# First feed-forward of a two-layer hybrid trunk: the fifth quad's weight forms made first, the norm taken later, and the rows of 1/rms made by two float32r products

## The chip, the cores and the metric

The kernel runs on one core of one Trainium2 chip. The metric is the device time of one execution in microseconds (us); three runs of the kernel before are given, and one execution was profiled.

## What is computed

Two layers, each a half-step SwiGLU feed-forward, a mixer of three head groups, and a second half-step feed-forward, all behind an RMS norm; a last RMS norm ends it. Here 512 positions of width 1024, feed-forward width 2816, all float32. The change is in the first feed-forward and in the norm that its six stages share.

```python
def _rmsnorm(x, g):
    y = xf * lax.rsqrt(jnp.mean(xf * xf, axis=-1, keepdims=True) + EPS)
    return (y * g.astype(jnp.float32)).astype(x.dtype)

def _swiglu(x, w_gate, w_up, w_down):
    return (jax.nn.silu(x @ w_gate) * (x @ w_up)) @ w_down

# in each layer
x = x + MACARON * _swiglu(_rmsnorm(x, ffn1_norm), ffn1_w_gate, ffn1_w_up, ffn1_w_down)
```

## The kernel before

**Tiling.** x stands transposed: 8 tiles of 128 features by 512 positions, held as four pairs `xp[m]`. A float32 product is made of three float32r products: each operand is split into a high part (a cast on ScalarE, L89) and a low part (a subtraction on VectorE, L90); `parts` is this pair. Every weight that reaches TensorE costs these two instructions.

**Quads.** The 22 column tiles of the gate and of the up matrix are taken in 22 *quads*: quad q covers two column tiles, of the gate for even q and of the up matrix for odd q. A quad is computed by a fast 2 by 2 block scheme: seven products n = 1 to 7 of half size (12 matmuls of 128x256 each, `product`, L281 to L283) in place of eight. Its weights come as raw blocks (`fetch`; for quad 4 of the very first feed-forward `fetch_apart`) and are made into forms in three steps (`forms_steps`): `direct` (tile `wd`, for n = 1, 2, 3), `first` (a sum, L148, and tile `wa`, for n = 7 and 6), `second` (a sum, L154, and tile `wb`, for n = 5 and 4). The tiles `wa` and `wb` share three buffers (tag `w2`), `wd` has two.

**Leaving PSUM.** After each product `after` copies or adds PSUM into the quad's tile `c`: n = 1 copies on ScalarE (L353), n = 2 adds on VectorE (L355), n = 6 and 5 copy on ScalarE (L357, L359), n = 7 and 3 subtract on VectorE (L361, L363), n = 4 copies on ScalarE (L365). n = 1, 6, 7 and 4 use one bank (`pa`), so n = 6 must wait for the copy after n = 1, and n = 7 for the copy after n = 6. Tiles `c` of even quads have the tag `g`, of odd quads `u`, two buffers each.

**The norm.** The features are not normalised before the product; the gate and up columns are multiplied by 1/rms afterwards. `squares(m)` squares a pair on ScalarE (L237, into a tile with the tag `u`) and adds it to `acc` on VectorE (two adds for each pair, the first pair one: seven adds, L240 and L243). `norm_columns` sums over partitions with four products with a column of ones (`pss`, L250) and takes the power on GpSimd (`rc`); `norm_rows` turns that into a tile of rows: four diagonals on VectorE (L264), four float32 products of 128x128 with a tile of ones (`psr`, L265), a copy (`rr`, L267). It is called six times in the program. `done(q)` then multiplies a gate by `rr` (L374), applies Silu, multiplies again (L376); for an odd quad it multiplies by the gate (L379) and splits the result into `h`.

**The first feed-forward.** In `start`, quads 0 and 1 are computed plainly (the `pg` products, while x and weights still arrive), with ScalarE's and VectorE's order written by hand up to the forms of quads 2 and 3. From there the order of the rest is set by the list `steps` in `gate_up` (times 7 q + `WHEN[n]`, some moved), by the list `norms` (one entry is called between the matmuls and the `after` of each product) and by a scheduler that puts each engine's instructions in a fixed order. The squares follow the copies of quads 0 and 1; `norm_columns` comes with the tenth product, `norm_rows` and `done(0)`, `done(1)` with the twelfth.

Of the kernel before, what the change touches and what calls it, by code (L numbers as in the profile page):

```python
# [9 lines left out]
F32 = mybir.dt.float32  # L10
F32R = mybir.dt.float32r
AF = mybir.ActivationFunctionType
ALU = mybir.AluOpType
AX = mybir.AxisListType

P = 128
D = 1024
T = 512
# [9 lines left out]
KP = KT // 2  # L28
# [20 lines left out]
def trunk(ctx, tc, xt, w_first, w_gu1, w_dn1, w_in, w_out, w_gu2, w_dn2, w_last, par, con, wst, bst, gvr, gain, out):  # L49
    nc = tc.nc  # L50
    cpool = ctx.enter_context(tc.tile_pool(name="cpool", bufs=1))
# [1 line left out]
    wpool = ctx.enter_context(tc.tile_pool(name="wpool", bufs=1))  # L53
    spool = ctx.enter_context(tc.tile_pool(name="spool", bufs=2))
    pp = ctx.enter_context(tc.tile_pool(name="pp", bufs=8, space=bass.MemoryType.PSUM))
    stage = {}

    def bank(name):
        return pp.tile([P, T], F32, tag="ps", name=name)
# [1 line left out]
    def big(name, dt=F32):  # L61
        return stage["pool"].tile([P, 2 * T], dt, tag="h", name=name, bufs=11)
# [3 lines left out]
    def uniq(s):  # L66
        uid[0] += 1
        return f"{s}{uid[0]}"
# [8 lines left out]
    ones = cpool.tile([P, P], F32, name="ones")  # L77
# [2 lines left out]
    nc.vector.memset(mhalf, -0.5)  # L80
    table = cpool.tile([P, 1], F32, name="table")
    nc.scalar.copy(table, mhalf[:, 0:1])
    ident = cpool.tile([P, P], F32, name="ident")
    make_identity(nc, ident)


    def parts(hi, lo, src):

        nc.scalar.copy(hi, src)  # L89
        nc.vector.tensor_tensor(lo, src, hi.bitcast(F32), ALU.subtract)  # L90

    def load(src):
        n = src.shape[-1] * (src.shape[1] if len(src.shape) == 3 else 1)
# [79 lines left out]
    split = parts  # L173


    state = {}
    warm_ps = bank("warm")
    xf = [None] * KP

# [6 lines left out]
    def xl(k):  # L186
        return xf[k // 2][:, 2 * T + (k % 2) * T : 2 * T + (k % 2 + 1) * T]

    def scratch(i, name):

        if stage["tags"] is None:
            return big(uniq(name))
        if i == 2:
            return stage["pool"].tile([P, 4 * T], F32, tag="hp", name=uniq(name), bufs=4)
        return stage["pool"].tile([P, 2 * T], F32, tag=stage["tags"][i], name=uniq(name), bufs=2)

    def gained(m, k, gcol, hi, lo, c):
# [59 lines left out]
    def norm_rows():  # L257

        rc = state["rc"]
        pr = bank(uniq("psr"))  # L260
        dg = scratch(2, "dg")
        for n in range(NCH):
            d = dg[:, n * P : (n + 1) * P]
            nc.vector.tensor_scalar(d, ident, rc[:, n : n + 1], None, ALU.mult)  # L264
            nc.tensor.matmul(pr[:, n * P : (n + 1) * P], lhsT=ones, rhs=d, start=True, stop=True)  # L265
        rr = spool.tile([P, T], F32, tag="rr", name=uniq("rr"), bufs=1)
        nc.scalar.copy(rr, pr)  # L267
        state["rr"] = rr
# [39 lines left out]
    def gate_up(w_gu, first, others, tail, from_start=False):  # L308
# [7 lines left out]
        quads = [(p, j) for p in range(FP) for j in range(2)]  # L316
        steps = [(7 * q + t, 0, q, n) for q in range(len(quads)) for n, t in WHEN.items()]
        if from_start:
            moved = {(3, 1): 15.3, (3, 2): 15.6, (2, 4): 27.5}
            steps = [(moved.get((q, n), t), k, q, n) for t, k, q, n in steps]  # L320
        steps += [(t, 1, None, work) for t, work in others]
        steps.sort(key=lambda e: e[:2])
        live, gates, raws = {}, {}, {}
# [25 lines left out]
        def after(q, n):  # L349
            c11, c21, c12, c22 = [quarter(q, i) for i in range(4)]  # L350
            b = live[q]
            if n == 1:
                state["copied"] = nc.scalar.copy(c11, b["pa"])  # L353
            elif n == 2:
                nc.vector.tensor_tensor(c11, b["pb"], c11, ALU.add)  # L355
            elif n == 6:
                state["copied"] = nc.scalar.copy(c12, b["pa"])  # L357
            elif n == 5:
                state["copied"] = nc.scalar.copy(c22, b["pc"])  # L359
            elif n == 7:  # L360
                nc.vector.tensor_tensor(c22, c22, b["pa"], ALU.subtract)  # L361
            elif n == 3:
                nc.vector.tensor_tensor(c12, b["pc"], c12, ALU.subtract)  # L363
            else:
                nc.scalar.copy(c21, b["pa"])  # L365
                done(q)

        def done(q):
            p, j = quads[q]
# [18 lines left out]
        else:  # L388
            begin(0)
            begin(1)  # L390
            for m in range(KP):
                for q in (0, 1):
                    for n in (1, 2):
                        ps = psum(q, ("pa", "pb")[n - 1])
                        hi, lo = live[q]["w"][n]
# [23 lines left out]
    def start(live, done, ahead, raws_of):  # L419

        for k in range(12):
            warm = warm_ps[:, (k % 4) * P : (k % 4 + 1) * P]
            nc.tensor.matmul(warm, lhsT=ones, rhs=ones, start=True, stop=True)
        pool = stage["pool"]
        extra = pool.tile([P, 4 * T], F32R, tag="hp", name="a21", bufs=4)
        a21 = [(extra[:, m * H : (m + 1) * H], extra[:, (4 + m) * H : (5 + m) * H]) for m in range(KP)]
        raws = [wpool.tile([P, 1024], F32, tag="pt", name=uniq("rawp"), bufs=3) for _ in range(KP - 1)]  # L430
        raws.append(wpool.tile([P, 12 * P], F32, tag="wdn", name=uniq("rawp"), bufs=2)[:, :1024])
        for k in (1, 0):
            nc.sync.dma_start(x[k], xt[:, k, :])
            nc.sync.dma_start(raws[0][:, (1 - k) * T : (2 - k) * T], w_first[0, :, (1 - k) * T : (2 - k) * T])
        for m in range(1, KP):
            nc.sync.dma_start(xp[m], xt[:, 2 * m : 2 * m + 2, :])
            nc.sync.dma_start(raws[m], w_first[m])
        ahead(2)
        ahead(3)
        ahead(4)  # L440
        ws, rooms = [], []
        steps2 = forms_steps(raws_of(2))
        steps3 = None
        with tc.manual_schedule(engines={mybir.EngineType.DVE, mybir.EngineType.Activation}):
            for m in range(KP):
                w = wpool.tile([P, 2048], F32R, tag="w2", name=uniq("wf"), bufs=3)
                ws.append(w)
                if m == 0:
                    parts(w[:, :T], w[:, 1024 : 1024 + T], raws[m][:, :T])
                norm_pair(m, G1, True)  # L450
                gained(m, 0, G1, a21[m][0], a21[m][1], slice(H, T))
                if m == 0:
                    parts(w[:, T:1024], w[:, 1024 + T :], raws[m][:, T:])
                else:
                    parts(w[:, :1024], w[:, 1024:], raws[m])
            for m in range(KP):
                r = pool.tile([P, 4 * T], F32, tag="hp", name=uniq("xw"), bufs=4)
                rooms.append(r)
                sums_of(m, G1, r[:, : 4 * H], r[:, 4 * H : 6 * H])
                if m:  # L460
                    sum_parts(m - 1, rooms[m - 1][:, : 4 * H])
                if m == 1:
                    steps2[1]()
            steps3 = forms_steps(raws_of(3))
            steps3[1]()
            sum_parts(KP - 1, rooms[KP - 1][:, : 4 * H])
            for f in steps2[2:] + steps3[2:]:
                f()
        ahead(5)
        ps = [[bank(uniq("pg")) for _ in range(2)] for _ in range(2)]  # L470
        for m in range(KP):
            kw = {"skip_group_check": True}
            for j in range(2):
                b11, b21, b22, b12 = [
                    [ws[m][:, o + j * T + i * P : o + j * T + (i + 1) * P] for o in (0, 1024)] for i in range(4)
                ]
                hi, lo = xf[m][:, H : 3 * H], xf[m][:, 8 * H : 10 * H]
                for i, w in ((0, b21), (1, b22)):
                    mm3(ps[j][i], w[0], w[1], hi, lo, m == 0, False, **kw)
                for i, w in ((0, b11), (1, b12)):  # L480
                    for t, a in ((slice(0, H), form(m, A11)), (slice(H, T), a21[m])):
                        mm3(ps[j][i][:, t], w[0], w[1], a[0], a[1], False, m == KP - 1, **kw)
        for j in range(2):
            c = pool.tile([P, 2 * T], F32, tag="gu"[j], name=uniq("gu"[j]), bufs=2)
            for i in range(2):
                nc.scalar.copy(c[:, i * T : (i + 1) * T], ps[j][i])
            live[j] = {"c": c}
        for j, w in ((0, steps2[0]), (1, steps3[0])):
            c = pool.tile([P, 2 * T], F32, tag="gu"[j], name=uniq("gu"[j]), bufs=2)
            live[2 + j] = {"w": w, "c": c}  # L490
        for m in range(KP):
            squares(m)

        def rows():
            norm_rows()
            done(0)
            done(1)

        wait = lambda: None
        return [wait] * 9 + [norm_columns, wait, rows]  # L500

    def schedule(l, w_dn, hs):

        def run(d, p0, p1):
            p = bank(uniq("pdn"))
# [18 lines left out]
        jobs = []  # L524
        for p0, p1 in CHUNKS[:-1]:
            for d in range(KT):
                t = 14 * p1 + 10 + 3.5 * d
                if p0:
                    jobs.append((t, lambda d=d, p0=p0, p1=p1: run(d, p0, p1)))
                else:  # L530
                    jobs.append((t - 10, lambda d=d: fetch_first(d)))
                    jobs.append((t - 4, lambda d=d: split_first(d)))
                    jobs.append((t, lambda d=d: run_first(d)))
        return jobs

    def ffn(l, w_gu, w_dn, after):
        with tc.tile_pool(name=uniq("ffn"), bufs=1, reuse_waits="tile") as pool:
# [6 lines left out]
                opened[d] = bank(uniq("pdn"))  # L544
                block_down(opened[d], l, w_dn, d, f0, hs[f0:f1], True, False)

            others = schedule(l, w_dn, hs)
            others += [(14 * p1 + t, lambda d=d: open_block(d)) for d, t in enumerate((0, 3, 6, 7))]

            def tail():  # L550
# [407 lines left out]
```

## Time and profile before

| | |
|---|---|
| three runs | 1816.51, 1817.7, 1818.04 us (median 1817.7) |
| profiled execution: its time | 1817.61 us |
| its span, first to last instruction | 1815.9 us |
| TensorE busy | 1802.4 us (99%) |
| VectorE busy | 1326.5 us (73%) |
| ScalarE busy | 826.1 us (45%) |

How to read it: the program is one long row of matmuls, and TensorE is busy nearly all of the span. A float32r matmul of 128x256 starts 0.12 us after the one before when the clock is at its upper level; a duration printed for one is longer than that, since matmuls overlap. So time is lost where the starts of two matmuls lie further apart than that: a wait, a slower product, or a stretch at the lower clock.

### The profile page before, as it was taken

The numbers are of one execution on the slowest core, as the hardware profiler recorded it, in microseconds if no ns is written. First come the engines' busy times: TensorE is split into PE (matmuls) and PEld (weight loads), VectorE is DVE, ScalarE is ACT, GpSimd is POOL, SyncE is SP. The second block draws the span as 40 slices with busy tenths as digits, with TensorE's granted clock in tenths as the row PEclk, the third lists the DMA queues.
The fourth block names the chain that finished last, engine by engine and source line by source line (L and its number), as shares of the span: only waits on it lengthen the run. The fifth ranks groups of instructions, "written<-read, shape, count | busy, mean of one in ns | idle before, by whom it ended". The sixth has DMA issues, their size and how long they took to land.

```text
span 1815.9 us, 28447 instructions
## 1 busy us (share of the span) xinstructions
PE 1802.4 (99%) x11576; PEld 1646.1 (91%) x11576; DVE 1326.5 (73%) x1828; ACT 826.1 (45%) x1224; POOL 121.0 (7%) x121
## 2 busy tenths in 40 slices
PE   9999999999999999999999999999999999999998
PEld 8999999888889999999899999998888899999996
DVE  8877777674687877777888777766657788777765
ACT  7544444413345544444554444434133455444443
POOL 1100000000100000000000000000000000000000
PEclk9999999999999999999999999999999999999999
DMA  7665655522223855556457555573322257565632
GB/s 244 164 160 153 153 145 150 176 81 93 70 82 82 223 145 151 150 156 157 128 129 197 148 152 148 152 190 115 98 70 70 70 144 196 151 155 157 157 88 82
DMA packets 120899, 251.19 MB, mean 138 GB/s; under 512 B 10048, under 2 KB 12352, under 8 KB 120512
## 3 DMA queue, kind: packets, MB, share of 16 engines
q1 hardware_dynamic: 97072, 204.02, 35.5%
q0 software_dynamic: 23408, 45.09, 15.3%
q8 instruction: 90, 1.47, 0.3%
q14 instruction: 41, 0.34, 0.1%
q10 hardware_dynamic: 288, 0.27, 0.0%
HBM read 247.25 MB, written 2.10 MB: 137 GB/s over the span
## 4 chain that ended last, share of the span: by engine, by line
PE 94%; DVE 4%; issue 1%; ACT 1%; DMA 0%; POOL 0%; SPq 0%; POOLq 0%; ACTq 0%; DVEq 0%
PE pa L281 9%; PE pa L282 9%; PE pa L283 9%; PE pdn L169 8%; PE pdn L170 8%; PE pdn L171 8%; PE pc L282 4%; PE pc L283 4%; PE pc L281 4%; PE pb L283 2%; PE pb L282 2%; PE pb L281 2%; PE pqk L169 2%; PE pqk L171 2%; PE pqk L170 2%; PE pout L171 2%
## 5 line engine op out<-in xcount | busy, mean ns | idle before, releaser
L169 PE MATMUL pdn<-h,wdn 128*128 128x512 f32 x632 | 247.6, 392 | 0.0
L170 PE MATMUL pdn<-h,wdn 128*128 128x512 f32 x632 | 247.6, 392 | 0.0
L171 PE MATMUL pdn<-h,wdn 128*128 128x512 f32 x632 | 246.0, 389 | 0.3 <-DVE wdn L90 0.3
L89 ACT CAST wd<-rawq 128x1024 fp32r<-128x1024 f32 (+1 forms) x170 | 133.4, 832 | 183.8 <-PE pc L283 170.3
L281 PE MATMUL pa<-xf,wa 128*128 128x256 f32 x688 | 195.7, 284 | 1.5 <-ACT g L353 1.5
L283 PE MATMUL pa<-xf,wa 128*128 128x256 f32 x688 | 195.3, 284 | 0.2 <-DVE wa L90 0.2
L282 PE MATMUL pa<-xf,wa 128*128 128x256 f32 x688 | 195.2, 284 | 0.0
L90 DVE TENSOR_TENSOR wd<-rawq,wd 128x1024 fp32r<-128x1024 f32 (+1 forms) x170 | 155.3, 954 | 48.6 <-ACT wd L89 48.4
L89 ACT CAST wdn<-rawd 128x512 fp32r<-128x512 f32 (+1 forms) x152 | 97.2, 639 | 176.2 <-PE pdn L171 173.5
L112 POOL DMA_DIRECT2D rawq<-in_w_gu x85 | 93.0, 1095 | 1241.7 <-DMA rawq<-in_w_gu 806.1
L89 ACT CAST w<-raw 128x1024 fp32r<-128x1024 f32 x77 | 80.9, 1051 | 205.3 <-PE pqk L171 60.6
L90 DVE TENSOR_TENSOR w<-raw,w 128x1024 fp32r<-128x1024 f32 x77 | 94.1, 1222 | 70.5 <-ACT w L89 69.8
L171 PEld LDWEIGHTS pdn<-h,wdn 128*128 128x128 f32 x632 | 118.7, 188 | 26.4 <-DVE wdn L90 0.7
L169 PEld LDWEIGHTS pdn<-h,wdn 128*128 128x128 f32 x632 | 119.2, 189 | 21.0
L170 PEld LDWEIGHTS pdn<-h,wdn 128*128 128x128 f32 x632 | 119.2, 189 | 19.5
L281 PEld LDWEIGHTS pa<-xf,wa 128*128 128x128 f32 x688 | 132.5, 193 | 2.6 <-ACT g L353 1.7
L283 PEld LDWEIGHTS pa<-xf,wa 128*128 128x128 f32 x688 | 132.6, 193 | 0.5 <-DVE wa L90 0.4
L90 DVE TENSOR_TENSOR wdn<-rawd,wdn 128x512 fp32r<-128x512 f32 (+1 forms) x152 | 107.0, 704 | 35.4 <-ACT wdn L89 35.4
L282 PEld LDWEIGHTS pa<-xf,wa 128*128 128x128 f32 x688 | 132.6, 193 | 0.0
L306 DVE SCALAR_TENSOR_TENSOR x<-pdn,x 128x512 f32<-128x512 f32 x152 | 103.8, 683 | 3.8 <-PE pdn L171 3.8
L90 DVE TENSOR_TENSOR wa<-rawq,wa 128x1024 fp32r<-128x1024 f32 x85 | 103.6, 1219 | 1.9 <-ACT wa L89 1.9
L90 DVE TENSOR_TENSOR wb<-rawq,wb 128x1024 fp32r<-128x1024 f32 x85 | 103.5, 1218 | 0.2 <-ACT wb L89 0.2
(283 smaller groups left out, 5041.1 us busy)
## 6 DMA issues: line engine op xcount, KB each, us to landing
rawq<-in_w_gu SPq DMA_DIRECT2D x170, 512.0 KB, 5.7
rawq<-in_w_gu POOLq DMA_DIRECT2D x85, 512.0 KB, 5.8
rawd<-in_w_dn SPq DMA_DIRECT2D x140, 256.0 KB, 4.5
raw<-in_w_in SPq DMA_DIRECT2D x52, 512.0 KB, 3.5
rawq<-in_w_gu SPq DMA_DIRECT2D x85, 256.0 KB, 6.0
raw<-in_w_out SPq DMA_DIRECT2D x16, 512.0 KB, 3.5
rawd<-in_w_dn SPq DMA_DIRECT2D x12, 384.0 KB, 3.2
raw<-in_w_last SPq DMA_DIRECT2D x6, 512.0 KB, 4.1
```

What stands on the lines that cost most here:

```text
L89: nc.scalar.copy(hi, src)
L90: nc.vector.tensor_tensor(lo, src, hi.bitcast(F32), ALU.subtract)
L112: nc.gpsimd.dma_start(two[:, :, 1, :], src.rearrange("p (n s c) -> p n s c", n=2, s=2)[:, :, 0, :], accum_op=ALU.add)
L169: nc.tensor.matmul(ps, lhsT=ah, rhs=bh, start=first, stop=False, **kw)
L170: nc.tensor.matmul(ps, lhsT=ah, rhs=bl, start=False, stop=False, **kw)
L171: nc.tensor.matmul(ps, lhsT=al, rhs=bh, start=False, stop=last, **kw)
L281: nc.tensor.matmul(ps, lhsT=hi[:, c], rhs=bh, start=one, stop=False, skip_group_check=True)
L282: nc.tensor.matmul(ps, lhsT=hi[:, c], rhs=bl, start=False, stop=False, skip_group_check=True)
L283: nc.tensor.matmul(ps, lhsT=lo[:, c], rhs=bh, start=False, stop=m == pairs[-1], skip_group_check=True)
L306: nc.vector.scalar_tensor_tensor(x[d], p, 0.5, x[d], ALU.mult, ALU.add)
```

## The change

- `norm_rows` (all six calls): each diagonal is made in two float32r parts (high by L265, low by a new scalar_tensor_tensor, L266), and two float32r products of 128x512 with `ones_r` take the place of the four float32 products of 128x128.
- `start`: the forms `first` and `second` of quad 4 are made right behind those of quads 2 and 3 (`steps4[1:]`); the tile `c` of quads 0 and 1 is one buffer of the tag `hp`, no longer one of `g` and one of `u`; the squares' VectorE adds are queued behind the last split of quad 4's forms (`issue_after`).
- `norms`: `norm_columns` with the sixteenth product, `norm_rows` with the eighteenth, then `done(0)` to `done(3)` one by one with the next four; quad 2's n = 4 is no longer moved to 27.5, and the first down-projection jobs come 7 units later in the list.

```diff
@@ norm_rows
-        dg = scratch(2, "dg")
+        d = scratch(2, "dp", F32R)
         for n in range(NCH):
-            d = dg[:, n * P : (n + 1) * P]
-            nc.vector.tensor_scalar(d, ident, rc[:, n : n + 1], None, ALU.mult)
-            nc.tensor.matmul(pr[:, n * P : (n + 1) * P], lhsT=ones, rhs=d, start=True, stop=True)
+            hi, lo = d[:, n * P : (n + 1) * P], d[:, T + n * P : T + (n + 1) * P]
+            nc.vector.tensor_scalar(hi, ident, rc[:, n : n + 1], None, ALU.mult)
+            nc.vector.scalar_tensor_tensor(lo, ident, rc[:, n : n + 1], hi.bitcast(F32), ALU.mult, ALU.subtract)
+        for i in range(2):
+            nc.tensor.matmul(pr, lhsT=ones_r, rhs=d[:, i * T : (i + 1) * T], start=i == 0, stop=i == 1)
@@ gate_up
-            moved = {(3, 1): 15.3, (3, 2): 15.6, (2, 4): 27.5}
+            moved = {(3, 1): 15.3, (3, 2): 15.6}
@@ after
-                done(q)
+                if not (from_start and q < 4):
+                    done(q)
@@ start
-            for f in steps2[2:] + steps3[2:]:
+            steps4 = forms_steps(raws_of(4))
+            for f in steps2[2:] + steps3[2:] + steps4[1:]:
                 f()
...
-            c = pool.tile([P, 2 * T], F32, tag="gu"[j], name=uniq("gu"[j]), bufs=2)
+            if j == 0:
+                c01 = pool.tile([P, 4 * T], F32, tag="hp", name=uniq("c"), bufs=4)
+            c = c01[:, 2 * j * T : 2 * (j + 1) * T]
...
-        for m in range(KP):
-            squares(m)
-
-        def rows():
-            norm_rows()
-            done(0)
-            done(1)
-
+        with tc.issue_after(state["split"].ins):
+            for m in range(KP):
+                squares(m)
         wait = lambda: None
-        return [wait] * 9 + [norm_columns, wait, rows]
+        gates = [lambda q=q: done(q) for q in range(4)]
+        return [wait] * 15 + [norm_columns, wait, norm_rows] + gates
@@ schedule
-                t = 14 * p1 + 10 + 3.5 * d
+                t = 14 * p1 + 10 + 3.5 * d + (0 if p0 else late)
```

Three places of the new order are spoken of below. In the names, the number behind `sq` rises with the pair m (41, 43, 44, 45 are pairs 0 to 3); `c37` is the tile of quads 0 and 1, `g38` that of quad 2, `u39` of quad 3, `g40` of quad 4, `u61` of quad 5; `wa27` and `wb28` are forms of quad 3, `wa30` and `wb31` of quad 4, `wa63` of quad 5; `pa48` is quad 3's bank and `pa52` quad 4's.

ScalarE in the first feed-forward, of the change, from the copy after quad 4's n = 1:

```order
L356 COPY g40_420<-pa52_599 128x256
L360 COPY g40_420<-pa52_599 128x256
L91 CAST wb31_256<-rawa8_132 128x1024
L238 ACTIVATE sq44_429<-x2_72 128x1024
L238 ACTIVATE sq45_433<-x3_73 128x1024
L356 COPY u39_419<-pa48_465 128x256
L362 COPY u39_419<-pc51_559 128x256
```

Before, all four squares stood ahead of quad 3's first copy with casts between them, and that copy came ahead of quad 4's `wa`. Now pairs 0 and 1 are squared at the very start, and pairs 2 and 3 stand between quad 4's `wb` and quad 3's first copy (L356).

VectorE at the same place, of the change:

```order
L92 TENSOR_TENSOR wb31_256<-rawa8_132,wb31_256 128x1024
L241 TENSOR_TENSOR acc42_423<-sq41_421 128x512
L244 TENSOR_TENSOR acc42_423<-acc42_423,sq43_425 128x512 x2
L244 TENSOR_TENSOR acc42_423<-acc42_423,sq44_429 128x512 x2
L244 TENSOR_TENSOR acc42_423<-acc42_423,sq45_433 128x512
L358 TENSOR_TENSOR u39_419<-pb49_479,u39_419 128x256
L244 TENSOR_TENSOR acc42_423<-acc42_423,sq45_433 128x512
```

Before, the seven adds stood one or two at a time between the sums and splits of quads 2 and 3. Now all seven stand behind the split of quad 4's `wb`.

TensorE, of the change, where quad 4's n = 7 ends:

```order
L286 MATMUL pa52_599<-xf16_167,wa30_252 128x256
L284 MATMUL pa52_599<-xf18_177,wa30_252 128x256
L285 MATMUL pa52_599<-xf18_177,wa30_252 128x256
L286 MATMUL pa52_599<-xf18_177,wa30_252 128x256
L284 MATMUL pa48_465<-xf12_147,wa27_237 128x256
L285 MATMUL pa48_465<-xf12_147,wa27_237 128x256
```

Before, quad 3's n = 6 and 7 came ahead of all of quad 4. Now quad 4's n = 1, 2, 6 and 7 come first, and the row behind them is quad 3's n = 6, which writes the bank `pa48` that quad 3's first copy has to have read.

## Rows read from the trace of the kernel before

**Rows 1.** The page: busy time of each engine and its share of the span.

```profile
PE 1802.4 (99%) x11576; PEld 1646.1 (91%) x11576; DVE 1326.5 (73%) x1828; ACT 826.1 (45%) x1224; POOL 121.0 (7%) x121
```

**Rows 2.** TensorE's waits in the first 100 us: who waited for whom, us, times, longest.

```profile
PE pa L281 <- ACT g L353: 1.5, 1, 1.5
...
PE pa L281 <- DVE g L361: 0.9, 1, 0.9
```

**Rows 3.** Busy time by stretch of the first feed-forward; columns in the first line.

```profile
core 0: us, PE busy (x) PEld busy (x) DVE busy (x) ACT busy (x) POOL busy (x), PEclk, DMA share, GB/s
...
46.00:47.00 1.00, 1.00 (x7) 1.00 (x7) 1.00 (x4) 0.00 (x0) 0.49 (x1) 0.50 0.77 78
...
61.00:62.00 1.00, 0.00 (x0) 0.00 (x0) 1.00 (x3) 0.90 (x1) 0.00 (x0) 1.00 0.00 0
...
60.00:80.00 20.00, 18.48 (x133) 17.25 (x133) 19.46 (x26) 12.71 (x20) 1.09 (x1) 1.00 0.32 103
```

**Rows 4.** TensorE's timeline, 29 to 49 us: start, duration, instruction, [idle before].

```profile
29.66 0.28 PE L281 MATMUL pa<-xf,wd 128*128 128x256 f32 x1
...
31.09 0.28 PE L281 MATMUL pb<-xf,wd 128*128 128x256 f32 x1
...
41.13 0.38 PE L281 MATMUL pc<-xf,wd 128*128 128x256 f32 x1 [0.23 <-ACT g L359]
...
42.55 0.28 PE L283 MATMUL pc<-xf,wd 128*128 128x256 f32 x1
43.72 0.39 PE L281 MATMUL pa<-xf,wb 128*128 128x256 f32 x1 [0.90 <-DVE g L361]
...
46.34 0.41 PE L281 MATMUL pa<-xf,wa 128*128 128x256 f32 x1
...
48.90 0.41 PE L283 MATMUL pc<-xf,wb 128*128 128x256 f32 x1
```

**Rows 5.** TensorE's timeline, 52 to 70 us.

```profile
52.23 1.05 PE L265 MATMUL psr<-dg,ones 128*128 128x128 f32 x8
53.04 0.36 PE L281 MATMUL pa<-xf,wd 128*128 128x256 f32 x1
...
60.67 0.28 PE L282 MATMUL pb<-xf,wd 128*128 128x256 f32 x1
62.47 0.39 PE L281 MATMUL pa<-xf,wa 128*128 128x256 f32 x1 [1.52 <-ACT g L353]
...
69.52 0.40 PE L169 MATMUL pdn<-h,wdn 128*128 128x512 f32 x1
69.75 0.40 PE L170 MATMUL pdn<-h,wdn 128*128 128x512 f32 x1
```

**Rows 6.** VectorE's timeline, 36 to 57 us.

```profile
36.53 1.41 DVE L243 TENSOR_TENSOR acc<-acc,sq 128x512 f32<-128x512 f32 x2
37.85 1.22 DVE L90 TENSOR_TENSOR wb<-rawq,wb 128x1024 fp32r<-128x1024 f32 x1
...
47.96 0.87 DVE L264 TENSOR_SCALAR dg<-ident,rc 128x128 f32<-128x128 f32 x4 [0.94 <-POOL rc L254]
...
54.18 2.35 DVE L374 TENSOR_TENSOR g<-g,rr 128x1024 f32<-128x1024 f32 x2
56.45 1.22 DVE L90 TENSOR_TENSOR wb<-rawa,wb 128x1024 fp32r<-128x1024 f32 x1
```

**Rows 7.** ScalarE's timeline: at 9 us, and from 41 to 54 us.

```profile
9.30 1.12 ACT L201 ACTIVATE xf<-x,pcol 128x512 fp32r<-128x512 f32 x2 [0.76 <-DMA x<-in_xt]
...
41.09 1.06 ACT L237 ACTIVATE sq<-x 128x1024 f32<-128x1024 f32 x1
...
43.39 1.04 ACT L89 CAST wb<-rawq 128x1024 fp32r<-128x1024 f32 x1
...
53.32 0.59 ACT L267 COPY rr<-psr 128x512 f32<-128x512 f32 x1 [0.32 <-PE psr L265]
53.80 0.38 ACT L365 COPY g<-pa 128x256 f32<-128x256 f32 x1
```

More of the change, by code (lines that the diff above doesn't have):

```diff
@@ L55, in trunk @@
     pp = ctx.enter_context(tc.tile_pool(name="pp", bufs=8, space=bass.MemoryType.PSUM))
-    stage = {}
+    stage, state = {}, {}
     def bank(name):
@@ L82, in trunk @@
     nc.scalar.copy(table, mhalf[:, 0:1])
+    ones_r = cpool.tile([P, P], F32R, name="ones_r")
+    nc.scalar.copy(ones_r, ones)
     ident = cpool.tile([P, P], F32, name="ident")
@@ L89, in parts @@
         nc.scalar.copy(hi, src)
-        nc.vector.tensor_tensor(lo, src, hi.bitcast(F32), ALU.subtract)
+        state["split"] = nc.vector.tensor_tensor(lo, src, hi.bitcast(F32), ALU.subtract)
     def load(src):
@@ L173, in trunk @@
     split = parts
-    state = {}
     warm_ps = bank("warm")
@@ L187, in xl, with scratch @@
         return xf[k // 2][:, 2 * T + (k % 2) * T : 2 * T + (k % 2 + 1) * T]
-    def scratch(i, name):
+    def scratch(i, name, dt=F32):
         if stage["tags"] is None:
-            return big(uniq(name))
+            return big(uniq(name), dt)
         if i == 2:
-            return stage["pool"].tile([P, 4 * T], F32, tag="hp", name=uniq(name), bufs=4)
+            return stage["pool"].tile([P, 4 * T], dt, tag="hp", name=uniq(name), bufs=4)
         return stage["pool"].tile([P, 2 * T], F32, tag=stage["tags"][i], name=uniq(name), bufs=2)
@@ L487, in start, with schedule @@
             live[j] = {"c": c}
-        for j, w in ((0, steps2[0]), (1, steps3[0])):
+        for q, w in ((2, steps2[0]), (3, steps3[0]), (4, steps4[0])):
+            j = q % 2
             c = pool.tile([P, 2 * T], F32, tag="gu"[j], name=uniq("gu"[j]), bufs=2)
-            live[2 + j] = {"w": w, "c": c}
-        for m in range(KP):
-            squares(m)
-        def rows():
-            norm_rows()
-            done(0)
-            done(1)
+            live[q] = {"w": w, "c": c}
+        with tc.issue_after(state["split"].ins):
+            for m in range(KP):
+                squares(m)
         wait = lambda: None
-        return [wait] * 9 + [norm_columns, wait, rows]
-    def schedule(l, w_dn, hs):
+        gates = [lambda q=q: done(q) for q in range(4)]
+        return [wait] * 15 + [norm_columns, wait, norm_rows] + gates
+    def schedule(l, w_dn, hs, late=0):
         def run(d, p0, p1):
@@ L545, in open_block @@
                 block_down(opened[d], l, w_dn, d, f0, hs[f0:f1], True, False)
-            others = schedule(l, w_dn, hs)
+            others = schedule(l, w_dn, hs, 7 if l == 0 and w_gu is w_gu1 else 0)
             others += [(14 * p1 + t, lambda d=d: open_block(d)) for d, t in enumerate((0, 3, 6, 7))]
```

## Prediction

> **What bounds the kernel now.** I read the page first, then TensorE's waits, then the timelines where the change acts. TensorE is busy for 1802.4 of 1815.9 us [rows 1], so almost any gain or loss must show as a change in how far apart the matmuls start. The list of waits finds only two over 0.5 us in the first feed-forward after the start [rows 2], 1.5 and 0.9 us. Undisturbed, twelve matmuls of 128x256 take 1.43 us, 0.12 each (29.66 to 31.09), but after 46 us the same twelve take 2.56, 0.21 each (46.34 to 48.90) [rows 4]: there the granted clock is 0.50, the 1.2 GHz level [rows 3]. VectorE is the engine behind it. From 60 to 80 us it works 19.46 of 20 us [rows 3], so whatever is put on it there makes something late.
>
> **1. Rows of 1/rms, six calls.** The four float32 products hold TensorE from 52.23 to 53.04, 0.81 us; two float32r products of 128x512 at the spacing of 69.52 to 69.75 take 0.46 [rows 5]. TensorE has no slack, so 6 x 0.35 = **-2.1 us**. VectorE gets four small instructions more in each call, 0.2 us each by the 0.87 for four like them [rows 6]. In five calls TensorE has other products in front of it and VectorE is 73% busy over the span [rows 1]: taken as nothing, at most 0.8 each without that cover. The cast of `ones` to `ones_r` falls in the start's idle time: nothing.
>
> **2. Before quad 4.** The seven adds to `acc` leave VectorE's work on quads 2 and 3. That helps only where an add stood ahead of what TensorE waits for. The wait at 41.13 is the trip from a product through ScalarE's copy to the next product: it stays. The one at 43.72 costs 1.17 - 0.12 = 1.05 (42.55 to 43.72), and there the subtraction (L361) stood behind an add; left is a trip like that at 41.13, idle 0.23 in place of 0.90 [rows 4]: **-0.7**. The stretch at 1.2 GHz follows this crowd of short waits and the four thin `pss` products. Some 17 matmuls of 0.21 in place of 0.12 make 1.6 us. With the waits shorter and `pss` gone from there, I take the stretch as gone: **-1.6** (0 to -1.6).
>
> Here a rule differs from the rows. The clock falls at 46 us though no idle before it was over 0.90 us, and it does not fall at 61 to 62, where TensorE idles the whole microsecond [rows 2, 3]. The Trainium skill (TensorE: Matmul & The Clock Gate, section "Why this matters for your kernels") lays a fall to one long idle gap between bursts of matmuls; by it this stretch would not hang on short waits, would stay, and the sum would be 1.6 us higher. The row decides: it shows the fall without the gap.
>
> Two squares (1.06 us each, [rows 7]) move to ScalarE's start, between the casts that feed the first products. ScalarE waited 0.76 us for x there [rows 7]; the rest of its delay falls on VectorE's and TensorE's stock of work. Nothing, at most 1.
>
> **3. Quad 4's forms earlier.** The wait of 60.67 to 62.47 was for quad 4's first copy, late behind other work on ScalarE: 1.80 - 0.12 = 1.68 goes [rows 5], **-1.7**. But quad 4's n = 6 and 7 now follow at once on its n = 1 and 2, with nothing between: n = 6 waits for the split of `wa30`, n = 7 for ScalarE's copy. Each lies between the trip at 41.13 (0.4) and the wait at 43.72 (1.05) [rows 4], so 0.8 to 2.1; I take **+1.3**.
>
> **4. The new long wait.** Behind quad 4's n = 7 TensorE's next product is quad 3's n = 6, which needs quad 3's first copy out of `pa48`. On ScalarE that copy now stands behind the cast of `wb31` and the squares of pairs 2 and 3. The cast of `wb31` needs a `w2` buffer: of the three, two hold quad 3's forms, still unused, and the third holds `wa30`, which is free only when quad 4's n = 7 has ended. The copy's own tile `u39` needs a buffer of the tag `u`; there are two. Pairs 0 and 1 hold them from the start. Pair 2's square gets pair 0's after the first add, pair 3's gets pair 1's after the third, and `u39` gets pair 2's after the fifth. All the adds stand behind the split of `wb31` on VectorE. So nothing of this can start before TensorE has run dry:
>
> - the last matmul's own end, 0.28 [rows 4];
> - cast of `wb31`, 1.04 [rows 7];
> - its split, 1.14 until the next VectorE instruction starts (two of this size take 54.18 to 56.45) [rows 6];
> - five adds, each on the sum before it, 1.41 for two [rows 6], so 3.5 (the squares of 1.06 fit beside two adds);
> - the copy, 0.38 [rows 7].
>
> Together 6.3, less the 0.12 of an undisturbed start and with some 0.1 for hand-overs: **+6.3** (6.0 to 6.8). No other row on TensorE can step in, since its order is fixed.
>
> **5. What is late next.** The sums of squares end only here, so `rr` comes late, and the four `done` fall among the forms of quads 5 and 6, on a VectorE that had 0.54 us to spare in 20 [rows 3]. Counted from the start of the `psr` products, TensorE has 0.46 + 48 x 0.12 = 6.2 us of work up to quad 5's n = 6. VectorE meanwhile: product and copy of `rr` (0.6 + 0.59 [rows 7]) with the split of `wd62` to about 1.7, then 1.14 for quads 0 and 1, 0.6 for half of `wd62`, 1.14 for quad 2, 1.14 again, 0.7 for the sum: 6.4; then ScalarE's cast, 1.04, to 7.5. TensorE waits about 1.3. Its third matmul needs the split, before which VectorE has another 1.14 and 0.6: 6.4 + 1.7 + 1.2 = 9.3, a second wait of about 1.4. That is 2.7. Quad 6's forms meet `done` of quads 2, 3 and 4 in the same way; I take 2.5 (0 to 5). **+5.2**.
>
> **6. Clock after the long wait.** Several microseconds with no matmul should put TensorE at 1.2 GHz once, for as long as the stretch that the trace has: **+1.6** (0 to 3.2).
>
> DMAs: their number is the same; quads 5 and 6 are fetched, as before, when `wb26` and `wb28` are split, and the power `rc` on GpSimd's queue now has quad 6's fetch ahead of it, issued long before. TensorE waits for no DMA in [rows 2]; nothing.
>
> **Sum:** -2.1 - 0.7 - 1.6 - 1.7 + 1.3 + 6.3 + 5.2 + 1.6 = **+8.3 us**. On the profiled execution's 1817.61 that is 1825.9; it lies 0.1 us under the median of the three runs, 1817.7, which gives **1826.0 us**.
>
> **Rivals.**
> - *The backlog does not form.* While TensorE waits, ScalarE and VectorE might catch up so far that step 5 and the low clock cost nothing: 8.3 - 5.2 - 1.6 = +1.5, 1819.2 us. For it: the long wait gives VectorE some time in which TensorE adds no work. Against it: VectorE spends it on the split and the adds of that very chain. Chance 0.10.
> - *The clock falls twice.* The waits of step 5 lie as close together as those around 42 to 44 us [rows 4]; one stretch more, or one twice as long, twice over: 8.3 + 3.2 = +11.5, 1829.2 us. Chance 0.12.
> - *Faster: the `u` and `w2` buffers do not bind.* If quad 3's first copy is not held back, steps 4 to 6 vanish, and quad 4's waits with them: -2.1 - 0.7 - 1.6 - 1.7 = -6.1, 1811.6 us. It decides whether TensorE idles over 1 us between quad 4's n = 7 and quad 3's n = 6. Against it speaks the fixed order. Chance 0.05.
>
> **How the numbers follow.** A measurement of this kernel can tell about 0.2%, 3.6 us, from no change. The forecast has 0.70 and its own range runs from 8.3 less half of step 5 and the whole of step 6 (+4.1) to +11; 0.03 is left for what I do not see. Low end 1821.0: a little below +4.1, with the backlog's rival left out. High end 1830.0: the second rival and the upper end of step 3. Slower by over 0.2%: 0.70 + 0.12 + 0.03 = 0.85; within: the first rival, 0.10; faster: 0.05.
>
> **What would show it.** One idle stretch of TensorE of 6 to 7 us near 53 to 59 us, ended by ScalarE's copy L356 of quad 3, with the cast of `wb`, its split and five adds end to end inside it: step 4. Two waits of about 1.3 us some 6 us behind the `psr` products: step 5. Granted clock 0.50 right after the long wait and none at 46 us: steps 6 and 2. `psr` at two records of 0.23 us spacing: step 1. I am wrong if no wait over 2 us appears, or if the time from 100 us on differs by more than step 1 gives.

## The result, and the profile after

The changed kernel takes **1827.2 us** (median of four runs, 1826.76 to 1827.65). The kernel before, beside it, takes 1817.8. The ratio is 1.0053 (95% interval 1.0036 to 1.0070): slower by 9.4 us, where 8.3 were forecast. The profiled execution took 1827.52 us, its span is 1825.8 (before 1815.9).

The page of the changed kernel, busy time of each engine; it answers to [rows 1]:

```profile
PE 1803.5 (99%) x11540; PEld 1644.3 (90%) x11540; DVE 1334.0 (73%) x1852; ACT 825.2 (45%) x1225; POOL 120.6 (7%) x121
```

By this row nothing has happened: TensorE works one microsecond longer in 1826. TensorE's waits in the first 100 us, against [rows 2]:

```profile
PE pa L284 <- ACT u L356: 6.5, 1, 6.5
PE pa L286 <- DVE wa L92: 2.4, 3, 1.1
PE pa L284 <- ACT wa L91: 1.5, 2, 0.8
...
PE pa L284 <- DVE g L364: 0.2, 1, 0.2
```

Of the two waits of [rows 2], that for ScalarE's copy has gone (1.5) and that for VectorE's subtraction has shrunk from 0.9 to 0.2 (L364). One of 6.5 us and a crowd of shorter ones have come. In TensorE's timeline of the changed kernel (start, duration, instruction, idle before and its releaser):

```profile
13.27 0.51 PE L173 MATMUL pg<-xf,wf 128*128 128x512 f32 x1 [0.52 <-DVE wf L92]
...
36.99 0.38 PE L286 MATMUL pa<-xf,wa 128*128 128x256 f32 x1 [0.76 <-DVE wa L92]
...
50.80 0.39 PE L286 MATMUL pa<-xf,wa 128*128 128x256 f32 x1 [0.49 <-DVE wa L92]
52.70 0.39 PE L284 MATMUL pa<-xf,wa 128*128 128x256 f32 x1 [0.46 <-ACT g L360]
...
54.12 0.28 PE L286 MATMUL pa<-xf,wa 128*128 128x256 f32 x1
60.87 0.58 PE L284 MATMUL pa<-xf,wa 128*128 128x256 f32 x1 [6.47 <-ACT u L356]
...
71.34 1.03 PE L268 MATMUL psr<-dp,ones_r 128*128 128x512 f32 x2
72.20 0.28 PE L284 MATMUL pa<-xf,wd 128*128 128x256 f32 x1
...
79.17 0.39 PE L284 MATMUL pa<-xf,wa 128*128 128x256 f32 x1 [0.79 <-ACT wa L91]
80.81 0.39 PE L286 MATMUL pa<-xf,wa 128*128 128x256 f32 x1 [1.13 <-DVE wa L92]
...
94.90 0.39 PE L284 MATMUL pa<-xf,wa 128*128 128x256 f32 x1 [0.73 <-ACT wa L91]
95.85 0.39 PE L284 MATMUL pc<-xf,wb 128*128 128x256 f32 x1 [0.44 <-ACT wb L91]
```

What stands inside the stretch from 54.12 to 60.87 is read on the other two engines. ScalarE's timeline, then VectorE's:

```profile
54.48 1.04 ACT L91 CAST wb<-rawa 128x1024 fp32r<-128x1024 f32 x1 [1.83 <-PE pa L286]
57.42 1.06 ACT L238 ACTIVATE sq<-x 128x1024 f32<-128x1024 f32 x1 [1.89 <-DVE acc L241]
58.87 1.06 ACT L238 ACTIVATE sq<-x 128x1024 f32<-128x1024 f32 x1 [0.40 <-DVE acc L244]
60.45 0.37 ACT L356 COPY u<-pa 128x256 f32<-128x256 f32 x1 [0.52 <-DVE acc L244]
```

```profile
55.56 1.22 DVE L92 TENSOR_TENSOR wb<-rawa,wb 128x1024 fp32r<-128x1024 f32 x1 [3.88 <-ACT wb L91]
56.70 0.69 DVE L241 TENSOR_TENSOR acc<-sq 128x512 f32<-128x512 f32 x1
57.42 3.74 DVE L244 TENSOR_TENSOR acc<-acc,sq 128x512 f32<-128x512 f32 x5
```

The releasers name the chain step by step: quad 4's n = 7 ends, ScalarE casts `wb`, VectorE splits it, the first add frees a `u` buffer for pair 2's square, later adds free one for pair 3's and one for quad 3's tile, and only then ScalarE copies quad 3's n = 1 and TensorE goes on. VectorE had idled 3.88 us before that split, with the adds queued behind it.

The windows, against [rows 3] (busy time and instructions of PE, PEld, DVE, ACT, POOL; then the granted clock, the DMA share, GB/s):

```profile
46.00:47.00 1.00, 1.00 (x10) 1.00 (x10) 1.00 (x3) 0.40 (x2) 0.38 (x1) 1.00 0.17 31
...
59.00:60.00 1.00, 0.00 (x0) 0.00 (x0) 0.97 (x2) 0.93 (x1) 0.00 (x0) 0.62 0.00 0
60.00:61.00 1.00, 0.13 (x1) 0.13 (x1) 0.90 (x2) 0.55 (x2) 0.00 (x0) 0.50 0.00 0
...
66.00:67.00 1.00, 1.00 (x10) 1.00 (x10) 0.13 (x1) 0.00 (x0) 0.00 (x0) 0.96 0.00 0
...
70.00:80.00 10.00, 8.86 (x65) 7.83 (x63) 10.00 (x18) 7.75 (x11) 0.00 (x0) 1.00 0.00 0
```

The clock, at the 1.2 GHz level near 46 us before, is at 1.00 there now, and at 0.50 from about 59.2 to 66.1 us. From 70 to 80 us VectorE has no idle time at all.

Where the time went is counted by the starts of the matmuls: each distance, less 0.119 us for a product of 128x256 and 0.23 for one of 128x512, is time lost (the `psr` and `pss` products are counted whole, each group in the stretch of the product that follows it).

| stretch of the profiled execution, us | lost before | lost after | difference |
|---|---|---|---|
| first product with x to 40: start, quad 2 begins | 1.71 | 3.16 | +1.45 |
| 40 to 53 | 4.35 | 2.58 | -1.77 |
| 53 to 68: the long wait and the low clock | 2.98 | 9.04 | +6.06 |
| 68 to 100 | 0.13 | 6.87 | +6.74 |
| 100 to 140 | 0.15 | 0.16 | +0.01 |

That is +12.5. The first product with x starts 0.5 us sooner (at 6.06, not 6.59), and the spans differ by 9.9; so some 2 us are won behind 140 us, where the other five calls of `norm_rows` lie. The first 140 us thus cost more than the whole change does.

### The profile page after: what moved, and what is told of

It is laid out like the page before. It is cut to its first block, busy times and chain, and to the rows that moved or that the text cites. A ratio compares the mean times of both kernels' runs of the same rounds, so it can differ in the third digit from the quotient of the medians.

```text
span 1825.8 us, 28404 instructions
## 1 busy us (share of the span) xinstructions
PE 1803.5 (99%) x11540; PEld 1644.3 (90%) x11540; DVE 1334.0 (73%) x1852; ACT 825.2 (45%) x1225; POOL 120.6 (7%) x121
## 3 DMA queue, kind: packets, MB, share of 16 engines
q8 instruction: 90, 1.47, 0.3%
## 4 chain that ended last, share of the span: by engine, by line
PE 93%; DVE 4%; ACT 1%; issue 1%; DMA 0%; POOL 0%; SPq 0%; POOLq 0%; ACTq 0%; DVEq 0%
PE pa L284 9%; PE pa L286 9%; PE pa L285 9%; PE pdn L171 8%; PE pdn L172 8%; PE pdn L173 8%; PE pc L285 4%; PE pc L286 4%; PE pc L284 4%; PE pb L285 2%; PE pb L284 2%; PE pb L286 2%; PE pqk L171 2%; PE pqk L173 2%; PE pout L172 2%; PE pout L171 2%
```

## The experiments

Each was timed beside the kernel before. "The change" is 1827.2 us. The median of the kernel before is 1817.2 to 1817.3 in these series and was 1817.8 beside the change, so a difference to the change carries some 0.6 us of doubt; smaller steps are read from the timelines.

### The long wait: which link binds

The squares' adds queued behind the split of quad 4's `wa`, one form earlier. The order of TensorE's products up to quad 3's n = 6 stays the same.

```diff
-            for f in steps2[2:] + steps3[2:] + steps4[1:]:
+            for i, f in enumerate(steps2[2:] + steps3[2:] + steps4[1:]):
                 f()
+                if i == 5:
+                    mark = state["split"]
...
-        with tc.issue_after(state["split"].ins):
+        with tc.issue_after(mark.ins):
```

> The seven adds of the squares are queued behind the split of quad 4's first form pair (wa) and no longer behind that of its second (wb); TensorE's own order is that of the change, instruction for instruction up to quad 3's n = 6. Theory (the adds stand behind a split that waits for TensorE to run dry, and quad 3's copy waits for the adds): the idle stretch of 6.47 us before quad 3's n = 6 shrinks to what is left of the chain on ScalarE, the matmul's end 0.28, the cast of wb 1.04 and the copy 0.38, less 0.12: about 1.6 us (1 to 2.5); the wait before quad 4's n = 7 may grow by up to one square, 1.06. The clock does not fall after it. Time: 1827.2 - 5 + 0.7 - 2.2 = about 1820.7 (1818.5 to 1823). Rival A (the w2 buffer, cast and split alone make the wait, the adds are hidden): still 3 us or more there, 1824 to 1827. Rival B (the clock falls whatever the length of the wait): wait 1.6 but the stretch at 0.50 stays, about 1823.

Measured: 1822.0 us (1820.52 to 1824.37), ratio 1.0027 (1.0017 to 1.0038). TensorE's timeline of this run, and VectorE's:

```profile
53.25 0.39 PE L284 MATMUL pa<-xf,wa 128*128 128x256 f32 x1 [1.09 <-ACT g L360]
56.40 0.39 PE L284 MATMUL pa<-xf,wa 128*128 128x256 f32 x1 [1.45 <-ACT u L356]
```

```profile
51.16 0.68 DVE L241 TENSOR_TENSOR acc<-sq 128x512 f32<-128x512 f32 x1
...
52.10 4.45 DVE L244 TENSOR_TENSOR acc<-acc,sq 128x512 f32<-128x512 f32 x6
56.47 1.22 DVE L92 TENSOR_TENSOR wb<-rawa,wb 128x1024 fp32r<-128x1024 f32 x1
```

The wait before quad 3's n = 6 is 1.45 us in place of 6.47, and the one before quad 4's n = 7 grew from 0.46 to 1.09, as the theory has it; rival A, which wanted 3 us or more, falls. The clock stayed up at 56 us, against rival B. But a stretch at 0.50 came later, from 74.2 to 77.6 us, and ate 1.3 us, which is what the time lies above the theory's middle. One window of this run, columns as above:

```profile
75.00:76.00 1.00, 1.00 (x7) 1.00 (x7) 1.00 (x2) 0.30 (x1) 0.00 (x0) 0.50 0.00 0
```

The other way round, with two more adds in the chain:

```diff
-            for i in range(2):
+            for i in (0, 1, 0, 1) if m == 1 and "few" in state else (0, 1):
                 nc.vector.tensor_tensor(state["acc"], state["acc"], sq[:, i * T : (i + 1) * T], ALU.add)
```

("few" is set only around the four calls of `squares` in `start`; the squares of pair 1 count double in the first norm.)

> The change, with the two adds of pair 1 made twice (that pair's squares count double in the first norm): two more adds of 128x512, 0.7 us each, in the chain behind the split of quad 4's wb, and nothing else. Theory (quad 3's copy waits for the fifth add): the idle stretch before quad 3's n = 6 grows from 6.5 to 7.9 us, the time by 1.4 to 1828.6, up to 1829.2 if what follows is later too. Rival (the copy waits for ScalarE's squares or for the cast, the adds run beside them): the stretch and the time stay, 1827.2 within 0.4.

Measured: 1828.4 us (1827.91 to 1828.87), +1.2 on the change. The wait, and the adds inside it:

```profile
62.06 0.58 PE L284 MATMUL pa<-xf,wa 128*128 128x256 f32 x1 [7.92 <-ACT u L356]
```

```profile
57.16 5.19 DVE L244 TENSOR_TENSOR acc<-acc,sq 128x512 f32<-128x512 f32 x7
```

7.92 against 6.47 is +1.45, two adds of 0.72. The copy waits for the adds; with the run above this settles step 4.

### The two squares at the start

The change, with the squares' ScalarE part queued behind the cast of quad 4's `wb` too:

```diff
-        nc.scalar.copy(hi, src)
+        state["cast"] = nc.scalar.copy(hi, src)
...
-        with tc.issue_after(state["split"].ins):
+        with tc.issue_after(state["split"].ins), tc.issue_after(state["cast"].ins):
```

> The change, with the squares of pairs 0 and 1 also taken out of ScalarE's start and queued behind the cast of quad 4's wb. Theory A (step 2 took those two squares at nothing; they are what makes the waits of 0.68 at 13.3 us and of 0.92 in place of 0.41 at 37 us): both go back, -1.2, about 1826.0; the long wait stays at 6.5, since the squares run beside the split of wb. Theory B (the wait at 13.3 us comes from the late landing of a weight load, and the one at 37 us from VectorE, whose adds were moved; the squares have room): 1827.2 within 0.5, with the 0.92 at 37 us still there. Theory C (the chain is bound by the squares too): the long wait grows by one square or two, 1828.2 or more.

Measured: 1827.1 us (1826.15 to 1827.44): no difference, which is theory B's number. Yet TensorE's timeline shows what theory A asked for, and where about half of it was given back:

```profile
35.65 0.39 PE L286 MATMUL pa<-xf,wa 128*128 128x256 f32 x1 [0.24 <-DVE wa L92]
...
59.93 0.58 PE L284 MATMUL pa<-xf,wa 128*128 128x256 f32 x1 [6.86 <-ACT u L356]
```

The wait at 37 us is 0.24 again (it was 0.76 in the change), that at 13 us is gone. The long wait grew by 0.39, since the cast of `wb` began 0.33 us later behind the last product than in the change (why was not settled), and 0.3 us more went at the low clock behind it (6.97 us from the end of the wait to the `pss` products, against 6.69). That is 0.7 of the 1.4 us won at the start; the two profiled executions still differ by 0.4 us (1827.08 against 1827.52), the medians by 0.1.

### The rows of 1/rms

The change with the old lines of `norm_rows`:

```diff
-        for i in range(2):
-            nc.tensor.matmul(pr, lhsT=ones_r, rhs=d[:, i * T : (i + 1) * T], start=i == 0, stop=i == 1)
+            nc.tensor.matmul(pr[:, n * P : (n + 1) * P], lhsT=ones, rhs=d, start=True, stop=True)
```

(and one diagonal for each n in place of two parts).

> The change with the old rows of 1/rms (four float32 products of 128x128 per call, four diagonals). Theory (step 1, TensorE has no slack, 0.35 us a call): five later calls give back 1.75 us, the first one 0.35 less what its four VectorE instructions cost in the backlog (0.8 at most): +1.3 to +2.1 on the change, 1828.5 to 1829.3. Rival (the four more VectorE instructions of each call cost elsewhere what TensorE saves): 1827.2 within 0.7.

Measured: 1829.0 us (1828.46 to 1829.23), +1.8 on the change (2.4 where each is held against the kernel before of its own series): the theory, and not its rival. The first call gives nothing: 0.86 us from 71.34 to 72.20 above, against 0.81 in this run:

```profile
71.12 1.05 PE L266 MATMUL psr<-dg,ones 128*128 128x128 f32 x8
71.93 0.36 PE L282 MATMUL pa<-xf,wd 128*128 128x256 f32 x1
```

In the change the second product waits there for the last low part, which VectorE works on from 71.20 (two of 128x128 in 0.60):

```profile
71.20 0.60 DVE L266 SCALAR_TENSOR_TENSOR dp<-ident,rc,dp 128x128 fp32r<-128x128 f32 x2
```

The other five calls, 0.35 each, are 1.75; behind 140 us, where they lie, all that is lost differs by 2.2 us between this run and the change.

### The clock behind the long wait

50 matmuls of 128x256 into the free half of quad 4's bank, behind its n = 7. They change what the bank holds for quad 4; the other work is that of the change.

```diff
             matmuls(q, n)
+            if from_start and (q, n) == (4, 7):
+                other = state["bank_pa4"][:, H:]
+                for i in range(50):
+                    nc.tensor.matmul(other, lhsT=ones_r, rhs=form(KP - 1, A11)[0], start=True, stop=True, skip_group_check=True)
```

> 50 float32r matmuls of 128x256 without use (into the unused half of quad 4's bank) are put behind quad 4's n = 7, into the long wait of the change: 50 x 0.12 = 6.0 us of the 6.5. Theory (step 6, the stretch at 0.50 behind the wait is the price of the idle TensorE): the wait shrinks to about 0.5, the granted clock stays 1.00 through 59 to 67 us, and 23 matmuls take 0.12 in place of 0.21: -2.2, 1825.0. Rival A (the clock is not what binds there: VectorE is so late from 68 us on that TensorE, 2.2 us sooner, only waits 2.2 us longer): clock 1.00 and still 1827.2. Rival B (the matmuls delay the copy or the cast): over 1828.

Measured: 1826.4 us (1826.10 to 1826.86), ratio 1.0052 against the 1.0053 of the change: at most 0.75 us won. What is left of the long wait is 0.48 us. Windows of this run, columns as above, and the two waits on TensorE's timeline that stand ahead of the second stretch:

```profile
59.00:60.00 1.00, 0.90 (x8) 0.69 (x6) 0.86 (x3) 0.48 (x2) 0.00 (x0) 1.00 0.01 2
...
79.00:80.00 1.00, 1.00 (x8) 1.00 (x7) 1.00 (x2) 0.28 (x1) 0.00 (x0) 0.58 0.00 0
80.00:81.00 1.00, 1.00 (x7) 1.00 (x7) 1.00 (x2) 0.37 (x1) 0.00 (x0) 0.50 0.00 0
```

```profile
76.65 0.39 PE L284 MATMUL pa<-xf,wa 128*128 128x256 f32 x1 [0.79 <-ACT wa L91]
...
78.28 0.39 PE L286 MATMUL pa<-xf,wa 128*128 128x256 f32 x1 [1.13 <-DVE wa L92]
```

Step 6's mechanism is shown: with TensorE kept busy, the clock stays up at 59 us. But neither theory nor rivals had what came: the low level appears 20 us later, behind the same pair of short waits (0.79 and 1.13) that the change passed at full clock, and costs 15 matmuls 1.4 us in all. In the profiles, 0.7 of the 2.1 us that the change loses at low clock are saved.

### The delay of the down-projection

The prediction named this line of the change in no step. Two runs price it: taken back in the change, and put back where no long wait is.

```diff
-            others = schedule(l, w_dn, hs, 7 if l == 0 and w_gu is w_gu1 else 0)
+            others = schedule(l, w_dn, hs, 0)
```

> Only the change's 7 units of delay for the first down-projection jobs are taken back; all else is the change. The prediction gave that delay no price. Theory A (between 70 and 96 us VectorE is the bound, and down-projection matmuls are work that TensorE can do without new forms, so moving them later takes cover away): the waits of 0.94, 1.29, 0.89 and 0.61 us at 79, 81, 95 and 96 us lose 1 to 3 us in sum, 1824.2 to 1826.2; the long wait of 6.5 us stays. Theory B (the late done of quads 0 to 3 alone make these waits; the place of the down-projection is indifferent): 1827.2 within 0.7.

Measured: 1825.9 us (1825.05 to 1826.58), -1.3: theory A, in its lower half. Against the series' own kernel before it is 0.7, which theory B would allow, so the time alone does not decide; the timeline does. The waits at 94.90 and 95.85 of the change are gone; those near 79 us stay (1.39, 0.47 and 0.16 in place of 0.79 and 1.13). A second stretch at low clock appears and takes 1.6 us (the first took 1.1, not 2.1), which hides some of the gain; windows of this run:

```profile
80.00:81.00 1.00, 0.84 (x4) 0.53 (x5) 1.00 (x2) 1.00 (x3) 0.00 (x0) 0.95 0.00 0
81.00:82.00 1.00, 1.00 (x7) 1.00 (x6) 1.00 (x2) 0.54 (x2) 0.00 (x0) 0.50 0.00 0
```

### Versions that beat both

First the kernel before with the new rows and quad 4's forms made early (with the tile `c` of quads 0 and 1 in `hp`), and of the norm's part only that `done(0)` and `done(1)` are called one by one. Against the change:

```diff
-        with tc.issue_after(state["split"].ins):
-            for m in range(KP):
-                squares(m)
+        for m in range(KP):
+            squares(m)
...
-        gates = [lambda q=q: done(q) for q in range(4)]
-        return [wait] * 15 + [norm_columns, wait, norm_rows] + gates
+        gates = [lambda q=q: done(q) for q in range(2)]
+        return [wait] * 9 + [norm_columns] + [wait] * 1 + [norm_rows] + gates
```

and quad 2's n = 4 at 27.5, `done(q)` for quads 2 and 3 and the down-projection as in the kernel before.

> The kernel before with quad 4's forms made early (and c of quads 0 and 1 in one buffer of hp) and the new rows of 1/rms, but with the squares where the kernel before lets them stand, the norm at its old place in the list and no delay of the down-projection. Theory (the loss of the change is the queueing of the squares and what follows from it; steps 1 and 3 by themselves are gains): no wait over 1.7 us, the wait of 1.52 at 62 us and the crowd at 70 to 96 us are gone; -2.1 of step 1, -1.7 of step 3, some 0.5 to 1 more in short waits at 34 to 41 us, and the stretch at 0.50 of 46 us stays somewhere: 1817.2 - 3 = 1814.2 (1812.5 to 1815.5). Rival (quad 4's forms early are the loss themselves: they take VectorE and ScalarE from quads 2 and 3): 1818 or more.

Measured: **1813.7 us** (1813.40 to 1815.56), ratio 0.9984 (0.9975 to 0.9993): faster than before, by 3.6 us, as the theory has it. Its number is partly luck: the waits at 34 to 41 us (TensorE's timeline) lose 2.8 us more than in the kernel before, where 0.5 to 1 was expected, but the wait of 1.05 us at 43.72 is gone, and so is the stretch at 0.50 that was expected to stay (from 8 to 100 us the clock is at 1.00):

```profile
34.67 0.39 PE L287 MATMUL pa<-xf,wd 128*128 128x256 f32 x1 [1.47 <-DVE wd L92]
38.08 0.39 PE L285 MATMUL pa<-xf,wa 128*128 128x256 f32 x1 [0.77 <-ACT wa L91]
39.34 0.38 PE L287 MATMUL pa<-xf,wa 128*128 128x256 f32 x1 [0.75 <-DVE wa L92]
```

Second the change with two edits, the mark of the first experiment at the first form of the list in place of the sixth, and no delay of the down-projection:

```diff
-                if i == 5:
+                if i == 0:
                     mark = state["split"]
...
-            others = schedule(l, w_dn, hs, 7 if l == 0 and w_gu is w_gu1 else 0)
+            others = schedule(l, w_dn, hs, 0)
```

> The change with two edits: the squares' adds are queued behind the split of quad 2's wa, the first of the forms in that list, in place of quad 4's wb, the last; and the down-projection is not delayed. Theory (with the adds early, two or three among the splits of quads 2 and 3, the third square's buffer is free early, quad 3's copy is not held, and the norm is ready long before the eighteenth product): no wait over 1.5 us; step 1 -2.1, the wait at 62 us -1.7, the long wait and the crowd at 70 to 96 us gone; one stretch at 0.50 may stay: 1811.5 to 1814.5, about 1813. Rival (the late place of the norm in the list makes VectorE's crowd whatever the squares do): the waits at 70 to 96 us stay, about 3 us, 1816 to 1818.

Measured: **1813.9 us** (1813.16 to 1814.34), ratio 0.9982 (0.9973 to 0.9991). The norm stands late in the list here as well, yet from 60 to 80 us TensorE works 19.07 of 20 us (windows of this run):

```profile
60.00:80.00 20.00, 19.07 (x135) 17.67 (x134) 18.79 (x25) 12.93 (x18) 1.14 (x1) 1.00 0.41 107
```

The scheduler's order is another one here: quad 3's n = 6 and 7 stand ahead of quad 4 again (all but one of its matmuls). So the order that I took as given in step 4 follows, at least in part, from where the squares are queued.

Then this version with the delay put back (`schedule` as in the change), so that the place of the squares is the one edit to the change:

> The run squares_first with the change's delay of the down-projection put back; that is the change with the place of the squares as its one edit. Theory A (moving down-projection matmuls later takes away work that TensorE has while VectorE makes forms, whether or not the norm is late): waits of 1 to 3 us in sum come back between 70 and 90 us, 1815 to 1817. Theory B (the delay only hurts behind the long wait; with the norm ready in time it is indifferent): 1813.9 within 0.7.

Measured: 1816.8 us (1816.36 to 1816.94): +2.9, theory A. The last two waits of the change's list stand there again, with no long wait and no low clock ahead of them; they are 1.5 of the 2.9 us:

```profile
84.03 0.39 PE L284 MATMUL pa<-xf,wa 128*128 128x256 f32 x1 [0.73 <-ACT wa L91]
84.98 0.39 PE L284 MATMUL pc<-xf,wb 128*128 128x256 f32 x1 [0.45 <-ACT wb L91]
```

Against the change this run differs by the squares' place alone: 1827.2 - 1816.8 = 10.4 us. The order of TensorE's products changes with it, so these 10.4 us are the price of both.

Last, squares_first with no square at the start:

```diff
-                    mark = state["split"]
+                    mark, mark2 = state["split"], state["cast"]
...
-        with tc.issue_after(mark.ins):
+        with tc.issue_after(mark.ins), tc.issue_after(mark2.ins):
```

> The run squares_first with the squares of pairs 0 and 1 also taken out of ScalarE's start: all four are queued behind the cast of quad 2's wa. Theory (the two squares at the start cost TensorE 0.5 to 0.7 us at 13 us and 0.5 at 37 us, and where no long wait follows, what is saved stays saved): those waits go back to 0 and 0.4, -1.0, about 1812.9 (1812.3 to 1813.5). Rival (as in squares_late, something later takes the gain back: the squares now stand ahead of the cast of quad 2's wb and of quad 3's forms): new waits at 38 to 45 us and 1813.9 or more.

Measured: **1813.3 us** (1812.60 to 1813.77), ratio 0.9978 (0.9969 to 0.9987), the lowest of all; 0.6 below squares_first, where 1.0 was expected, and the ranges overlap. The wait at 37 us went from 0.76 to 0.27. But at 13 us there was one in this profile without any square at the start, where ScalarE waits for loads; TensorE's timeline, then ScalarE's:

```profile
13.56 0.50 PE L173 MATMUL pg<-xf,wf 128*128 128x512 f32 x1 [0.53 <-DVE wf L92]
```

```profile
7.81 0.62 ACT L91 CAST wf<-rawp 128x512 fp32r<-128x512 f32 x1 [0.94 <-DMA rawp<-in_w_first]
9.79 1.12 ACT L202 ACTIVATE xf<-x,pcol 128x512 fp32r<-128x512 f32 x2 [1.35 <-DMA x<-in_xt]
```

## Why the prediction was right, step by step

**Step 4 carried it and was right in mechanism and size**: +6.3 forecast; 60.87 - 54.12 = 6.75, less 0.12, is 6.6. Every link of the chain is in the timelines, and the two runs on the adds show that it binds.

**Step 1**: -2.1 forecast, -1.8 to -2.4 measured by undoing it; in the profiles -1.75 by the products' own times, -2.0 by all that is lost behind 140 us. Five calls give the 0.35 each; the first gives nothing, because VectorE was late there. "At most 0.8 without that cover" was the right warning, put on the wrong calls: it was the first that lost its cover.

**Step 2**: the loss of 1.05 at 43.72 fell to 0.33, as forecast, and the stretch at 0.50 near 46 us is gone. That it went because the short waits and the `pss` products went is not shown: quad4_only has longer waits at 34 to 41 us and its `pss` products at 47, and no such stretch. The term that was mis-sized is "Nothing, at most 1" for the two squares at the start. They cost 0.5 us at 37 us: both runs without them bring that wait back to 0.24 or 0.27. The 0.7 at 13 us in the change's profile is another matter. It lies between 0 and 0.7 among profiles with the squares (none in filler) and without (none in squares_late, 0.7 in no_square_at_start), so it does not need them; ScalarE waits longest for its second load where it is 0.7 (1.19 us in the change, 0.94 in no_square_at_start, 0.44 in filler, 0.75 in squares_late). How much of it the squares add in the change was not separated.

**Step 3**: the wait of 1.68 at 62 us is gone, as forecast; for n = 6 and 7, +1.3 forecast, 0.65 + 0.62 = 1.27 measured, by a split and a copy as named.

**Step 5**: the size was right, the account incomplete. Of the 6.87 us lost between 68 and 100 us, 0.81 are the `pss` and 0.86 the `psr` products, both counted elsewhere; 5.2 are left, and +5.2 was forecast. That the two agree so well is partly luck. Two waits, 0.79 and 1.13, stand 7.8 and 9.5 us behind the `psr` products, where two of about 1.3 were expected some 6 behind; they lose 2.2, of 2.7 forecast. But I laid all of it to the late `done` calls. The delay of the down-projection, which no step named, costs 2.9 us by itself (squares_first_down_later) and 0.7 to 1.3 in the change. The two waits at 94.90 and 95.85, which lose 1.7 with the slow starts behind them where 2.5 were put on quad 6's forms and `done`, are its own: they go when it is taken back, and come when it is put into a kernel without the long wait.

**Step 6**: +1.6 forecast, 2.1 measured: 22 matmuls by 0.095. By the granted clock the stretch lasted 6.8 us, twice the 3.4 of the kernel before, but TensorE was still idle for its first 1.6 us: so it cost more than that of [rows 3], and not twice as much.

**The rivals.** The backlog did form. The clock fell once in the change; it fell twice in down_not_later, so that rival was close; nothing here shows why it fell only once in the change, and that part of the forecast is luck. The faster rival did not come, but its point of decision was the right one: where the buffers do not bind, as in squares_first (which leaves out the delay too), the kernel is faster than before, by 3.4 us against the 6.1 of the rival's sum, which left out the squares at the start and what I had not seen, losses of 0.9 at 39.7 and 1.0 at 70.5 us.

Between the two profiled executions the forecast was 8.3 and the difference is 9.9. Missing are 0.5 for the squares at 37 us, 0.7 at 13 us, 0.5 at low clock, 0.3 in step 4 and 0.1 to 0.3 in step 1; against them stands the start, 0.5 sooner.

## What to carry to other kernels

Where work is queued behind an instruction by hand, ask what that instruction waits for, and whose buffers the queued work holds: here adds that nobody needed soon stood behind a split that could not start before TensorE ran dry, and held the buffer that TensorE's next product needed. Price every line of a change, also a constant in a list of times: here work that was moved later had covered TensorE where VectorE was full. And a change of several parts is worth taking apart: two of its parts were gains of some 3.5 us, hidden under one queueing decision of 10.

## What the runs showed of the hardware that I had not expected

In two runs the low clock moved rather than went away. With the long wait filled (filler) or shortened to 1.45 us (adds_earlier), the granted clock stayed at 1.00 there and then fell at 79.2 and 74.2 us, with no wait of TensorE over 1.13 us behind 61 us: in both, the waits of 0.79 and 1.13 stand just ahead of it. The change passed the same two waits, 0.79 and 1.13, at 79.17 and 80.81 at full clock. In quad4_only three waits of 1.47, 0.77 and 0.75 within 5 us went by with no fall. So the length of one wait does not tell it; what does is open.

The Trainium skill (TensorE: Matmul & The Clock Gate, section "Why this matters for your kernels") ties a fall to one long idle gap between bursts of matmuls. The fall inside the change's 6.5 us agrees with that; those of the kernel before, of filler and of adds_earlier come with no wait over 1.5 us ahead of them, and there the measurement decides: a long gap is not the only way to a fall.
